# A diffusion backbone on one core: three modulation chunks move from TensorE to VectorE, and the rest is tied to its place

## The chip, the cores and the metric

The kernel runs on one core of one Trainium2 chip. The metric is the device time of one execution in microseconds; the time before is the median of three executions.

## The reference

Two layers of a diffusion backbone over 256 latent tokens and 256 context tokens, 2048 channels, float32. Each layer is a token mixer and then a gated MLP with a centred depthwise convolution of width 3. Every sub-layer reads a normalised and modulated stream. Layer 0 mixes by centred pooling in four channel groups, layer 1 by neighbourhood attention. Cut to what matters:

```python
ml = (silu_c  @ w_mod[i] + b_mod[i]).reshape(B, 6, 1, D)      # latent stream
mc = (silu_cc @ w_mod[i] + b_mod[i]).reshape(6, 1, 1, D)      # context stream
a_lat = modulate(rms_norm(h, norm1_g[i]), ml[:, 0], ml[:, 1]) # x * (1 + scale) + shift
# layer 0: window mean minus itself, then a 512 x 512 product per group
y_lat = pool_mix(a_lat, pool_w[j], pool_b[j], pool_scale[j])
h = h + ml[:, 2] * y_lat
h = h + ml[:, 5] * conv_ffn(modulate(rms_norm(h, norm2_g[i]), ml[:, 3], ml[:, 4]),
                            ffn_w_gate[i], ffn_w_up[i], ffn_conv_w[i], ffn_conv_b[i], ffn_w_down[i])
```

The context stream hc goes the same way with mc. For each layer the modulation is a vector of 2048 for each stream times a 2048 x 12288 matrix: six vectors (shift, scale and gate of the first norm, then of the second).

## The kernel before, in words

Channels lie on the partitions in 16 tiles (KT) of 128, hl and hc holding the two streams. Large products run in pairs of rounded float32 halves: a weight tile is loaded by SP's queue (load), cast on ScalarE into a high part and subtracted on VectorE into a low part (split, lines 172 and 174), and each product is three matmuls.

**The modulation of layer 0.** w_mod's 12288 columns are cut into 24 chunks of 512; chunk 4*w + g is vector w of channel group g (w = 3 is the second norm's shift, so chunks 12 to 15). mod_pe makes a chunk on TensorE: four pieces of two loads each (128 x 1024, 512 KB), and after each second piece a batch of 16 matmuls in four column strips (line 240), which waits until its four loads are whole. After the second batch ScalarE copies the accumulator (line 255), four transposes (line 262) bring it onto partitions, and VectorE adds up and applies bias and gain (lines 264, 217, 219). mod_pe is a generator with one pump step per piece. mods() puts the chunks in order: for each group g the chunks g, 4 + g, 8 + g, 16 + g, 12 + g, then 20 to 23, so 96 steps. need(n) pumps up to step n. shifts(g) copies a finished chunk 12 + g into the small tile sh (line 531). Layer 1's modulation is made later, while the MLP runs, by mod_pairs: VectorE adds up w_mod row by row (lines 298 and 300), transposes and reduces (310 and 311), and TensorE sums four quarters (quarter_sum, line 201).

**The partial stage.** The second norm's scale over channels is known only when all four groups have been mixed, so the MLP's first eight output tiles (NS, two products each, gate and up) are begun group by group without the norm: partial(g) multiplies group g's unnormalised tiles Ad (lines 705 to 707, 12 matmuls per output tile and product) and adds the result into part (line 718, VectorE). The norm's factor is applied at the end (late), and the shift's share of the product comes from its own small products pw of the weights with sh (line 687), transposed at line 721. While partial(g) runs, between(half) is called 32 times, once every six matmuls; each call pumps the modulation up to a step that grows with half (LEAD, RATE, PMAX), lets the next group's mixer take a step when its chunks are there (todo), lends buffers to the loads (lend, LENT), and in group 3 makes the second norm's factor (n2.rstd) and starts the normalised tiles A (normalise) and the first gates (GATES). The mixer of group g + 1 makes window sums on VectorE, its products on TensorE (lines 574 to 576), adds on GpSimd (line 635) and makes the Ad of the next group (lines 645 and 646).

**Order.** The program is emitted in this order, and a planner then orders each engine's instructions by a simulated time and by priorities. tc.issue_after(x) keeps an instruction behind x on the same engine; behind_of holds such an x for the modulation on TensorE, and is empty in the partial stage before. Loads are issued by SP in turn, each as soon as its buffer is free.

Of the kernel before, what the change touches and what calls it, by code (L numbers as in the profile page):

```python
# [33 lines left out]
LEAD = 18  # L34
RATE = 20
PMAX = 30

# [22 lines left out]
def kernel(ctx: ExitStack, tc: tile.TileContext, xT, cxT, wmod, wg, wu, wd, wp,  # L60
# [96 lines left out]

    casts = []

    def split(ts, name, share=0, keep=False):  # L160

        parts = []
        for j, (t, n) in enumerate(ts):
# [5 lines left out]
            with ExitStack() as behind:  # L169
                for ins in hold:  # L170
                    behind.enter_context(tc.issue_after(ins))
                casts.append(nc.scalar.copy(hi[:, :n], t[:, :n]).ins)  # L172
                eng = nc.gpsimd if share and turn[0] % share == 0 else nc.vector
                eng.tensor_tensor(lo[:, :n], t[:, :n], hi[:, :n].bitcast(F32), op=ALU.subtract)  # L174
            parts.append((hi, lo))
# [148 lines left out]
    class Norm:  # L324
# [51 lines left out]

        def rstd(self):
            nj = self.n // P
            ps = bank("d", f"{self.name}s")
# [9 lines left out]
            for j in range(nj):  # L389
                nc.vector.tensor_scalar(dg[:, P * j : P * j + P], ident, v[:, j : j + 1], None, op0=ALU.mult)  # L390
            pb = bank("d", f"{self.name}b")
            nc.tensor.matmul(pb[:, : self.n], ones, dg[:, : self.n], start=True, stop=True)
            return pb
# [36 lines left out]
    with ExitStack() as ph0:  # L430
# [64 lines left out]
        with ExitStack() as phs:  # L495
# [37 lines left out]
            def mods():  # L533

                for g in range(4):
                    for w in (0, 1, 2, 4):
                        yield from mod_pe(0, 4 * w + g, sc, f0)
                    yield from mod_pe(0, 12 + g, sc, f0)
                    shifts(g)
                for q in range(4):  # L540
                    yield from mod_pe(0, 20 + q, sc, f0)

            pump0 = mods()
            done = [0]

            def need(n):
                while done[0] < n:
                    next(pump0, None)
                    done[0] += 1
# [110 lines left out]
            def partial(g, sh, between):  # L660

                step = 0
                for fa in range(0, NS, 4):
                    for q, (nm, wsrc) in enumerate((("g", wg), ("u", wu))):
# [12 lines left out]
                        for j in range(4):  # L677
                            f = fa + j
                            between(2 * step)
                            if j == (3 if fa == 0 and q == 0 else 0):  # L680
                                need(20 * g + 21)
                                assert g in READY
# [19 lines left out]
                            for i in range(4):  # L702
# [3 lines left out]
                                nc.tensor.matmul(ps, hi[:, c : c + P], xl, start=False, stop=False)  # L706
                                nc.tensor.matmul(ps, lo[:, c : c + P], xh, start=False, stop=(final and i == 3))
                                if i == 1:
# [33 lines left out]
            with tc.issue_after(fetched[-1]):  # L742
                nc.sync.dma_start(vt[1], vec[:, NFIRST:])
            rstd = None
            for g in range(4):
                if g < 3:
                    lend((range(8, KT), [*range(12, KT), *range(4)], range(8))[g])
                mix = mixer(g + 1) if g < 3 else None
                todo = [20 * g + 20 + n for n in STEPS] if g < 3 else []
                last = [14]  # L750
# [3 lines left out]
                def between(half):  # L754
                    need(min(20 * g + LEAD + RATE * (half + 1) // 32, 20 * g + LEAD + PMAX))
                    if (g, half) in LENT:
                        lend(LENT[g, half])
                    if g == 3 and half == NRH:
                        nc.scalar.copy(rstd, n2.rstd())
                        late_norm.append(rstd)  # L760
                        need(20 * g + 21)
                    if todo and done[0] > todo[0] and half >= last[0] + 2:
                        last[0] = half
                        todo.pop(0)
                        next(mix)
                    k = (half - NRH) // 2
                    if g == 3 and 0 <= k < 12 and (half - NRH) % 2 == 0:
# [8 lines left out]
                for n in todo:  # L776
                    need(n)
                    next(mix)
            need(97)
            in_turn.clear()  # L780
# [768 lines left out]
```

## Time and the profile before

| | us |
|---|---|
| median of 3 executions | 3037.05 |
| lowest, highest | 3035.22, 3038.11 |
| the profiled execution, its own time | 3037.08 |
| its span, first to last instruction | 3035.3 |
| TensorE busy in the span | 2972.4 |
| mean granted TensorE clock | 0.995 |

The profile is one execution. PE is TensorE's matmuls, PEld its weight loads, DVE VectorE, ACT ScalarE, POOL GpSimd, SP the queue that issues the loads. A row of the timeline gives start, length, engine, line, operation, output <- inputs, and in brackets how long the engine stood idle before it and what released it. A clock of 1.00 is full speed.

### The profile page before, as it was taken

What the parts mean: (1) busy time and instruction counts of PE and PEld (TensorE: products, weight loads), DVE (VectorE), ACT (ScalarE), POOL (GpSimd) and SP (SyncE); (2) the same over time, 40 slices, a digit from 0 to 9 for tenths busy, and PEclk for the clock granted to TensorE, in tenths of its full rate; (3) what the DMA queues carried; (4) which work ended last, traced back from release to release, by engine and by line L of the source; (5) the groups of instructions that cost most, each with busy time, mean ns of one, the idle gap of its engine ahead of it and who ended that gap; (6) DMA issues with size and microseconds to landing.
All of it is one profiled execution on the core that took longest, in us unless ns stands there. A gap on an engine that the chain in (4) does not pass through costs nothing.

```text
span 3035.3 us, 40942 instructions
## 1 busy us (share of the span) xinstructions
PE 2972.4 (98%) x15132; PEld 2414.0 (80%) x15132; DVE 1943.6 (64%) x2782; ACT 1380.5 (45%) x2237; POOL 833.1 (27%) x819
## 2 busy tenths in 40 slices
PE   5999999999999999999999999999999999999998
PEld 2666568888888888888888887878888888888887
DVE  5455664386584857758485657474778666666666
ACT  4433454323333242333434534343556666566665
POOL 0000213303123030311305002020002566566665
PEclk9999999999999999999999999999999999999999
DMA  9798563374665847566482333333345555555563
GB/s 395 290 366 306 209 209 103 109 252 146 208 197 168 245 140 236 156 205 203 156 254 82 127 100 122 107 120 112 106 158 195 185 193 191 190 183 187 183 192 119
DMA packets 178935, 561.81 MB, mean 185 GB/s; under 512 B 17712, under 2 KB 22576, under 8 KB 178736
## 3 DMA queue, kind: packets, MB, share of 16 engines
q1 hardware_dynamic: 178736, 559.19, 56.5%
q8 instruction: 120, 1.97, 0.3%
q14 instruction: 79, 0.65, 0.1%
HBM read 557.03 MB, written 2.10 MB: 184 GB/s over the span
## 4 chain that ended last, share of the span: by engine, by line
PE 88%; issue 6%; DMA 2%; POOL 1%; DVE 1%; ACT 1%; SPq 0%; DVEq 0%; POOLq 0%; ACTq 0%
PE d L863 5%; PE d L864 5%; PE d L865 5%; PE u L1070 5%; PE g L1070 5%; PE d L1123 4%; PE g L807 4%; PE g L805 4%; PE g L806 4%; PE u L807 4%; PE u L805 4%; PE u L806 4%; PE u L1073 3%; PE g L1073 3%; PE d L1127 2%
## 5 line engine op out<-in xcount | busy, mean ns | idle before, releaser
L876 POOL TENSOR_TENSOR hl<-hl,dy 128x256 f32<-128x256 f32 x160 | 146.1, 913 | 945.8 <-ACT dy L875 945.6
L1139 POOL TENSOR_TENSOR hl<-hl,dy 128x256 f32<-128x256 f32 x320 | 332.1, 1075 | 188.3 <-ACT dy L1137 186.0
L300 DVE SCALAR_TENSOR_TENSOR macc<-wm,sc,macc 128x512 f32<-128x512 f32 (+1 forms) x360 | 328.7, 943 | 75.3 <-DMA wm<-wmod 74.3
L875 ACT ACTIVATE dy<-d,modT 128x256 f32<-128x256 f32 x320 | 133.1, 469 | 187.3 <-PE d L865 168.9
L876 POOL TENSOR_TENSOR hc<-hc,dy 128x256 f32<-128x256 f32 x160 | 129.4, 809 | 0.0
L174 DVE TENSOR_TENSOR wd_2l<-wd,wd_2h 128x1024 fp32r<-128x1024 f32 (+1 forms) x44 | 55.7, 1271 | 108.1 <-ACT wd_2h L172 106.9
L1137 ACT ACTIVATE dy<-d,modT 128x512 f32<-128x512 f32 x160 | 104.5, 684 | 43.0 <-PE d L1127 41.4
L240 PE MATMUL mod<-wm,sc 128*32 128x512 f32 x768 | 99.6, 629 | 9.9 <-DMA wm<-wmod 9.9
L1225 POOL TENSOR_TENSOR rk<-rk,rp 128x256 f32<-128x256 f32 x16 | 14.8, 926 | 324.0 <-DVE rk L1224 225.6
L174 DVE TENSOR_TENSOR wd_3l<-wd,wd_3h 128x1024 fp32r<-128x1024 f32 (+1 forms) x44 | 53.4, 1234 | 77.1 <-ACT wd_3h L172 75.7
L635 POOL TENSOR_TENSOR hl<-hl,pz 128x256 f32<-128x256 f32 x12 | 9.8, 820 | 286.9 <-ACT pz L633 286.9
L174 DVE TENSOR_TENSOR wd_1l<-wd,wd_1h 128x1024 fp32r<-128x1024 f32 (+1 forms) x44 | 53.7, 1225 | 53.3 <-ACT wd_1h L172 53.3
L172 ACT CAST wd_1h<-wd 128x1024 fp32r<-128x1024 f32 (+1 forms) x44 | 45.3, 1031 | 72.3 <-PE u L806 47.1
L174 DVE TENSOR_TENSOR wd_0l<-wd,wd_0h 128x1024 fp32r<-128x1024 f32 (+1 forms) x44 | 54.5, 1247 | 36.9 <-ACT wd_0h L172 36.9
L1314 ACT ACTIVATE sb<-sb,nm 128x512 f32<-128x512 f32 x64 | 46.3, 723 | 58.9 <-DVE nm L1310 57.3
L172 ACT CAST wd_0h<-wd 128x1024 fp32r<-128x1024 f32 (+1 forms) x44 | 45.0, 1031 | 54.5 <-PE u L1070 29.1
L1102 DVE TENSOR_TENSOR actb<-sgb,actb 128x256 fp32r<-128x256 f32 x43 | 50.8, 1180 | 26.0 <-ACT actb L1101 26.0
L480 ACT ACTIVATE sg<-g 128x512 f32<-128x512 f32 x43 | 27.2, 632 | 88.4 <-DVE g L477 88.3
L863 PE MATMUL d<-act,wd_2h 128*128 128x512 f32 x172 | 67.1, 390 | 0.0
L864 PE MATMUL d<-act,wd_2h 128*128 128x512 f32 x172 | 66.9, 389 | 0.0
L865 PE MATMUL d<-act,wd_2l 128*128 128x512 f32 x172 | 66.9, 389 | 0.0
L864 PE MATMUL d<-act,wd_0h 128*128 128x512 f32 x172 | 66.9, 389 | 0.0
(1778 smaller groups left out, 9304.8 us busy)
## 6 DMA issues: line engine op xcount, KB each, us to landing
wm<-wmod SPq DMA_DIRECT2D x384, 512.0 KB, 6.5
wd<-wd SPq DMA_DIRECT2D x168, 512.0 KB, 4.4
wg<-wg SPq DMA_DIRECT2D x156, 512.0 KB, 4.7
wu<-wu SPq DMA_DIRECT2D x156, 512.0 KB, 4.6
wv<-wv SPq DMA_DIRECT2D x32, 512.0 KB, 4.0
wk<-wq SPq DMA_DIRECT2D x32, 512.0 KB, 3.9
wq<-wq SPq DMA_DIRECT2D x32, 512.0 KB, 3.8
wo<-wo SPq DMA_DIRECT2D x32, 512.0 KB, 4.4
```

The costliest lines, as they stand in the source:

```text
L174: eng.tensor_tensor(lo[:, :n], t[:, :n], hi[:, :n].bitcast(F32), op=ALU.subtract)
L300: nc.vector.scalar_tensor_tensor(acc[s], v, sc2[:, k, s : s + 1], acc[s], op0=ALU.mult, op1=ALU.add)
L805: nc.tensor.matmul(ps, hi[:, c : c + P], xh, start=(k == 0), stop=False)
L806: nc.tensor.matmul(ps, hi[:, c : c + P], xl, start=False, stop=False)
L807: nc.tensor.matmul(ps, lo[:, c : c + P], xh, start=False, stop=(k == KT - 1))
L863: nc.tensor.matmul(ps, hi[:, o : o + P], xh, start=(i == 0), stop=False)
L864: nc.tensor.matmul(ps, hi[:, o : o + P], xl, start=False, stop=False)
L865: nc.tensor.matmul(ps, lo[:, o : o + P], xh, start=False, stop=(i == n - 1))
L876: nc.gpsimd.tensor_tensor(h_of(s)[:, k, :], h_of(s)[:, k, :], y[:, s], op=ALU.add)
L1070: nc.tensor.matmul(ps, hi[:, c : c + P], flat(B[k]), start=(k == 0), stop=False)
L1073: nc.tensor.matmul(ps[:, T:], lo[:, c : c + P], B[k][:, 0], start=False, stop=(k == KT - 1))
L1139: nc.gpsimd.tensor_tensor(hl[:, k, :], hl[:, k, :], y[:, q], op=ALU.add)
```

## The change

Chunks 13, 14 and 15 no longer go through mod_pe. added_up makes them on VectorE during partial(0), partial(1) and partial(2): 16 rows of 512 columns for each of the two streams, each row a multiply-add into the accumulator macc0 (a seventh tile of the ring act), then per stream a transpose and a reduction, and quarter_sum on TensorE. The rows are kept behind the last low-part subtraction that VectorE was given (vector_last). It takes a step every 0.8 half-steps, from half-step 10 in group 0 and from 3 in groups 1 and 2. mods() then has 84 steps, 16 for each of the groups 1 to 3; the pace is 20 steps per group in group 0 and 16 after. behind_of now always holds the last matmul of the partial products, so that modulation matmuls and transposes stay behind the place at which they are emitted. The second norm's factor is made in two parts, the sums and the diagonal at half-step 3 and the spreading matmul, tied in the same way, at half-step 5; the normalised tiles start one step later, and group 3 no longer waits for chunk 15.

```diff
@@ -32,8 +32,8 @@
 NC = 6
 
 LEAD = 18
-RATE = 20
-PMAX = 30
+RATE0 = 20
+RATE = 16
 
 NRH = 3
 GATES = (16, 19, 22, 25)
@@ -156,6 +156,7 @@
         return ts
 
     casts = []
+    vector_last = []
 
     def split(ts, name, share=0, keep=False):
 
@@ -171,7 +172,9 @@
                     behind.enter_context(tc.issue_after(ins))
                 casts.append(nc.scalar.copy(hi[:, :n], t[:, :n]).ins)
                 eng = nc.gpsimd if share and turn[0] % share == 0 else nc.vector
-                eng.tensor_tensor(lo[:, :n], t[:, :n], hi[:, :n].bitcast(F32), op=ALU.subtract)
+                ins = eng.tensor_tensor(lo[:, :n], t[:, :n], hi[:, :n].bitcast(F32), op=ALU.subtract)
+                if eng is nc.vector:
+                    vector_last[:] = [ins.ins]
             parts.append((hi, lo))
         if not keep:
             used(ts)
@@ -375,6 +378,10 @@
             return pb
 
         def rstd(self):
+            self.diagonal()
+            return self.spread_all()
+
+        def diagonal(self):
             nj = self.n // P
             ps = bank("d", f"{self.name}s")
             for i, sq in enumerate((self.acc, self.last)):
@@ -388,8 +395,14 @@
             dg = self.pool.tile([P, 512], F32, tag="t2", name=f"{self.name}d")
             for j in range(nj):
                 nc.vector.tensor_scalar(dg[:, P * j : P * j + P], ident, v[:, j : j + 1], None, op0=ALU.mult)
+            self.dg = dg
+
+        def spread_all(self, last=()):
             pb = bank("d", f"{self.name}b")
-            nc.tensor.matmul(pb[:, : self.n], ones, dg[:, : self.n], start=True, stop=True)
+            with ExitStack() as behind:
+                for x in last:
+                    behind.enter_context(tc.issue_after(x))
+                nc.tensor.matmul(pb[:, : self.n], ones, self.dg[:, : self.n], start=True, stop=True)
             return pb
 
     A = {}
@@ -535,10 +548,45 @@
                 for g in range(4):
                     for w in (0, 1, 2, 4):
                         yield from mod_pe(0, 4 * w + g, sc, f0)
-                    yield from mod_pe(0, 12 + g, sc, f0)
-                    shifts(g)
+                    if g == 0:
+                        yield from mod_pe(0, 12, sc, f0)
+                        shifts(0)
                 for q in range(4):
                     yield from mod_pe(0, 20 + q, sc, f0)
+
+            def added_up(ch, acc):
+
+                for k in range(KT):
+                    if k % 2 == 0:
+                        g, j = divmod(k, 4)
+                        ts = load(lambda a, b: wmod[0, ch, g, :, 512 * j + a : 512 * j + b], 1024, f"wv{ch}_{k}")
+                        t = ts[0][0]
+                    with ExitStack() as behind:
+                        for x in vector_last:
+                            behind.enter_context(tc.issue_after(x))
+                        v = t[:, 512 * (k % 2) : 512 * (k % 2) + 512]
+                        for s in both:
+                            if k == 0:
+                                nc.vector.tensor_scalar(acc[:, s], v, sc2[:, k, s : s + 1], None, op0=ALU.mult)
+                            else:
+                                nc.vector.scalar_tensor_tensor(acc[:, s], v, sc2[:, k, s : s + 1], acc[:, s],
+                                                               op0=ALU.mult, op1=ALU.add)
+                    if k % 2:
+                        used(ts)
+                    yield
+                r = st.tile([P, 16, 2], F32, tag="modr", bufs=2, name=f"modr0_{ch}")
+                for s in both:
+                    t = f0.tile([P, 512], F32, tag="t2", name=f"modu{s}_0_{ch}")
+                    nc.vector.transpose(t, acc[:, s])
+                    nc.vector.tensor_reduce(out=r[:, :, s], in_=t.rearrange("p (k r) -> p k r", r=32), axis=AX.X, op=ALU.add)
+                    yield
+                yield
+                with ExitStack() as behind:
+                    for x in behind_of:
+                        behind.enter_context(tc.issue_after(x))
+                    src = quarter_sum(r, 2, f"modt_0_{ch}")
+                finish_mod(0, ch, both, src)
+                shifts(ch - 12)
 
             pump0 = mods()
             done = [0]
@@ -678,7 +726,8 @@
                             f = fa + j
                             between(2 * step)
                             if j == (3 if fa == 0 and q == 0 else 0):
-                                need(20 * g + 21)
+                                if g == 0:
+                                    need(21)
                                 assert g in READY
                                 pw = bank("d", f"pw{nm}{g}_{fa}")
                                 for i in range(4):
@@ -704,7 +753,8 @@
                                 xh, xl = flat(A[4 * g + i][:, 0]), flat(A[4 * g + i][:, 1])
                                 nc.tensor.matmul(ps, hi[:, c : c + P], xh, start=(first and i == 0), stop=False)
                                 nc.tensor.matmul(ps, hi[:, c : c + P], xl, start=False, stop=False)
-                                nc.tensor.matmul(ps, lo[:, c : c + P], xh, start=False, stop=(final and i == 3))
+                                ins = nc.tensor.matmul(ps, lo[:, c : c + P], xh, start=False, stop=(final and i == 3))
+                                behind_of[:] = [ins.ins]
                                 if i == 1:
                                     between(2 * step + 1)
                             step += 1
@@ -742,28 +792,39 @@
             with tc.issue_after(fetched[-1]):
                 nc.sync.dma_start(vt[1], vec[:, NFIRST:])
             rstd = None
+            summed = act_tile("macc0", F32)
             for g in range(4):
                 if g < 3:
                     lend((range(8, KT), [*range(12, KT), *range(4)], range(8))[g])
                 mix = mixer(g + 1) if g < 3 else None
-                todo = [20 * g + 20 + n for n in STEPS] if g < 3 else []
+                todo = [16 * g + 20 + n for n in STEPS] if g < 3 else []
+                adding = [added_up(13 + g, summed)] if g < 3 else []
+                taken = [0]
                 last = [14]
                 F = {}
                 rstd = n2.acc
 
                 def between(half):
-                    need(min(20 * g + LEAD + RATE * (half + 1) // 32, 20 * g + LEAD + PMAX))
+                    if g == 0:
+                        need(LEAD + RATE0 * (half + 1) // 32)
+                    else:
+                        need(LEAD + 4 + RATE * g + RATE * (half + 1) // 32)
+                    while adding and (half - (3 if g else 10)) * 10 >= 8 * taken[0]:
+                        taken[0] += 1
+                        if next(adding[0], "end") == "end":
+                            adding.pop()
                     if (g, half) in LENT:
                         lend(LENT[g, half])
                     if g == 3 and half == NRH:
-                        nc.scalar.copy(rstd, n2.rstd())
+                        n2.diagonal()
+                    if g == 3 and half == NRH + 2:
+                        nc.scalar.copy(rstd, n2.spread_all(behind_of))
                         late_norm.append(rstd)
-                        need(20 * g + 21)
                     if todo and done[0] > todo[0] and half >= last[0] + 2:
                         last[0] = half
                         todo.pop(0)
                         next(mix)
-                    k = (half - NRH) // 2
+                    k = (half - NRH) // 2 - 1
                     if g == 3 and 0 <= k < 12 and (half - NRH) % 2 == 0:
                         normalise(0, 3, h_of, both, rstd, f0, range(k, k + 1), keep=F)
                     if g == 3 and half == 24:
@@ -776,7 +837,8 @@
                 for n in todo:
                     need(n)
                     next(mix)
-            need(97)
+            need(85)
+            behind_of.clear()
             in_turn.clear()
             nbank[0] = 0
             A.update(F)

```

## The prediction

> **What bounds the kernel now.** I read the page first, then the busy time by stage, PE's timeline in the partial stage, the waits, and VectorE's timeline.
>
> ```profile
> span 3035.3 us, 40942 instructions
> PE 2972.4 (98%) x15132; PEld 2414.0 (80%) x15132; DVE 1943.6 (64%) x2782; ACT 1380.5 (45%) x2237; POOL 833.1 (27%) x819
> PE 88%; issue 6%; DMA 2%; POOL 1%; DVE 1%; ACT 1%; SPq 0%; DVEq 0%; POOLq 0%; ACTq 0%
> ```
>
> PE is busy for 98% of the span and makes 88% of the chain that ended last. Work taken from PE in the stage that changes shortens the run, unless PE then waits. That stage runs from 69 to 417 us. Its first three groups are cut in two below; the last row is the head of group 3. Columns: stretch, length, busy time of PE, PEld, DVE, ACT and POOL (instructions in brackets), granted clock, DMA share, GB/s.
>
> ```profile
> 69.40:107.76 38.36, 37.60 (x237) 22.68 (x237) 13.11 (x24) 16.67 (x31) 0.00 (x0) 1.00 1.02 393
> 107.76:158.20 50.44, 48.02 (x281) 32.48 (x280) 28.30 (x55) 24.21 (x45) 6.28 (x8) 1.00 0.66 229
> 158.20:194.00 35.80, 35.58 (x205) 23.07 (x205) 12.89 (x26) 9.09 (x15) 0.00 (x0) 0.95 1.01 389
> 194.00:246.00 52.00, 52.00 (x313) 32.98 (x311) 35.47 (x69) 21.92 (x41) 6.39 (x8) 1.00 0.79 280
> 246.00:280.70 34.70, 34.70 (x213) 22.09 (x209) 14.15 (x27) 9.38 (x16) 0.00 (x0) 1.00 1.00 372
> 280.70:331.10 50.40, 49.45 (x293) 32.46 (x293) 36.15 (x70) 21.61 (x41) 5.95 (x8) 1.00 0.72 264
> 331.10:376.50 45.40, 39.05 (x221) 24.63 (x219) 26.86 (x55) 15.44 (x35) 10.53 (x8) 0.92 0.59 202
> ```
>
> PE is full in groups 0 to 2. The DMA engines are full in the first half of each group and free for a fifth to a third of the second. VectorE works 140.1 of 261.7 us in the three groups (the six rows added), so 121.6 us are idle. Group 3's head is where PE loses most: 6.4 us idle and a clock of 0.92.
>
> **What comes off PE.** Chunks 13 to 15 lose their matmuls and transposes. One batch of 16 matmuls, and one set of four transposes, in PE's timeline:
>
> ```profile
> 270.09 0.60 PE L262 MATMUL modt<-ident,modev 128*128 128x128 f32 x4
> 270.62 1.92 PE L240 MATMUL mod<-wm,sc 128*32 128x512 f32 x16
> ...
> 276.46 0.39 PE L707 MATMUL cu<-Ad,wcu_0l 128*128 128x512 f32 x1
> 276.78 1.92 PE L240 MATMUL mod<-wm,sc 128*32 128x512 f32 x16
> 278.64 0.50 PE L705 MATMUL cu<-Ad,wcu_0h 128*128 128x512 f32 x1
> 278.98 0.40 PE L706 MATMUL cu<-Ad,wcu_0h 128*128 128x512 f32 x1
> 279.22 0.40 PE L707 MATMUL cu<-Ad,wcu_0l 128*128 128x512 f32 x1
> ```
>
> From L707 at 276.46 to L707 at 279.22 are 2.76 us. Three steps between ordinary matmuls take 0.23 us each (the pitch of undisturbed neighbours, about the 0.24 of the last two rows), so one batch costs 2.07 us. The transposes cost 0.53 (270.09 to 270.62). A chunk is two batches and one set, 4.67 us; three are 14.0 us. All of it stands in PE's full stretches. Each chunk now ends with a sum over four quarters on PE, which layer 1 already shows:
>
> ```profile
> L201 PE MATMUL modt_0s<-modr,quad x2: 191/232/274, 637.6 to 637.6; 128*128 128x32 f32 x2
> ```
>
> Two matmuls of 0.23 are 0.46 us, 1.4 for three; at the lower bound they vanish between neighbours. I take 1.4. Net: 12.6 us less.
>
> **Two waits that lose their cause.** Group 3 now has the last batch of chunk 15 in front of its first shift sums:
>
> ```profile
> 343.54 0.16 DVE L386 TENSOR_SCALAR n2v<-n2v 128x4 f32<-128x4 f32 x1
> 345.18 3.64 PE L240 MATMUL mod<-wm,sc 128*32 128x512 f32 x16 [4.64 <-DMA wm<-wmod]
> 345.34 0.86 DVE L390 TENSOR_SCALAR n2d<-ident,n2v 128x128 f32<-128x128 f32 x4
> 348.75 2.02 PE L392 MATMUL n2b<-n2d,ones 128*128 128x512 f32 x2
> 355.32 0.16 DVE L531 COPY sh<-modT 128x8 f32<-128x8 f32 x1
> 355.63 1.09 PE L687 MATMUL pwg<-wcg,sh 128*32 128x256 f32 x16 [1.65 <-ACT A L405]
> ...
> 345.20:350.60 5.40, 5.40 (x18) 1.37 (x19) 1.01 (x5) 0.00 (x0) 0.00 (x0) 0.50 0.97 333
> ```
>
> PE stands 4.64 us for that batch's weights and then runs 5.4 us at a clock of 0.50, 2.7 us lost: together 7.3. The shift of group 3 is copied at 355.32, and pwg, which reads it, starts right after, 1.65 us late (the view names ACT, but that copy came last). After the change chunk 15 is summed during group 2 and need(81) is gone, so these 9.0 us lose their cause.
>
> What is late next there is the second norm. Its diagonal is ready at 346.2 (345.34 and 0.86), because L386 came only at 343.54; from there the chain is 2.7 us long. The spreading matmul is now tied two half-steps after the sums: 12 matmuls of 0.23 and a batch of 2.07, 4.8 us of cover. If L386 comes as promptly as that needs, the wait is nothing; if it is again held up, the chain from the sums to the diagonal,
>
> ```profile
> 337.13 0.28 PE L382 MATMUL n2s<-ones,n2q 128*128 128x1 f32 x2
> ```
>
> is 9.1 us against 4.8, a wait of 4.3 and half a slow stretch like the one above, 6.5 in all. I take 3.3, the middle: nothing in the rows says which. Later normalisation by one step and the last 14 of 84 pump steps in group 3 cost nothing: PE's own matmuls hide them.
>
> **What VectorE gets.** A chunk is 32 rows, two transposes and two reductions, all seen in layer 1:
>
> ```profile
> 602.99 4.71 DVE L300 SCALAR_TENSOR_TENSOR macc<-wm,sc,macc 128x512 f32<-128x512 f32 x7
> L310 DVE STREAM_TRANSPOSE modu<-macc x32: 657/682/705, 626.0 to 1636.5; 128x512 f32<-128x512 f32 x32
> L311 DVE TENSOR_REDUCE modr<-modu x32: 634/654/677, 627.2 to 1638.4; 128x16 f32<-128x512 f32 x32
> DVE macc L300 <- DMA wm<-wmod: 74.3, 63, 4.0
> ```
>
> Seven rows take 4.71 us, 0.67 each; 32 are 21.5, the rest 2.7: 24.2 us a chunk, 72.6 for three. Of 121.6 us idle 49.0 remain, and 36.4 once PE's share of the stage is 12.6 shorter. So the work fits, in groups 1 and 2 in half-steps 3 to 19, before the mixers crowd the second half.
>
> The new wait is that of a row for its weights. Behind it in VectorE's queue stand the additions into part (L718) that free PE's accumulators, the splits, and the mixer. Layer 1 waits 1.2 us a time (74.3 over 63); 24 loads at that are 28.3 us, inside the 36.4. So I charge PE only where slack is short: at the change of groups, where PE waits for Ad.
>
> ```profile
> 158.20 0.73 PE L705 MATMUL cg<-Ad,wcg_0h 128*128 128x512 f32 x2 [2.42 <-ACT Ad L645]
> 158.20:162.60 4.40, 4.17 (x11) 2.98 (x12) 3.61 (x9) 2.65 (x7) 0.00 (x0) 0.64 0.96 336
> ```
>
> That gap is 2.4 us and 4.4 us at a clock of 0.64, 1.6 more: 4.0. There are three changes of group. Between none of them and three extra gaps (12.0), and 4.0 of gain if this one goes, I take one, 4.0.
>
> On the clock the Trainium skill ("TensorE: Matmul & The Clock Gate", Part 1) says that it drops after an idle window of some 3.4 us. By that rule the 2.4 us gap would have cost itself alone and the sum would be 1.6 lower; the trace shows a clock of 0.64 behind 2.42 us, and the measurement decides.
>
> The 24 loads replace 24 loads, so bytes stay. Group 0 gets chunk 13's 4.2 MB (8 loads of 128 x 1024 fp32) on top of what it had; SP's queue puts them ahead of wp and wcg. The row 107.76 to 158.2 moves 229 GB/s where the first moves 393: 8.3 MB of room. Three evictions fewer on ACT and the tie itself (an order on PE that the trace mostly has already) I cost at nothing; PE's matmuls hide the first, and where the tie makes a transposed chunk late it is one of the gaps above.
>
> **Sum.** The profiled execution took 3037.08 us, the median is 3037.05. 3037.08 - 12.6 - 9.0 + 3.3 + 4.0 = 3022.8, so 3023.
>
> **Rivals.** *All gaps go.* With the norm prompt and the gap at 158.2 closed by the earlier mixer: 3037.08 - 12.6 - 9.0 - 4.0 = 3011.5. For it: groups 1 and 2 have 16 pump steps instead of 20, so by the code their mixers start some three half-steps earlier. Against: VectorE is fuller.
>
> *The gaps come back.* The norm waits 6.5 and each change of group has one more gap: 3015.5 + 6.5 + 12.0 = 3034.0, no change that a measurement tells (it tells 0.2%, 6 us). For it: VectorE's rows fill just the idle time that kept the boundary short.
>
> *VectorE's queue stands.* Weights come late to the row at its head, additions behind it stop, and PE runs out of accumulators.
>
> ```profile
> ACT wcg_4h L172 <- DMA wcg<-wg: 19.8, 6, 7.1
> ```
>
> In this stage a cast that waits for weights waits 3.3 us (19.8 over 6). 24 loads at 3.3 are 79.2, 42.8 above the 36.4 idle: 3015.5 + 42.8 = 3058. It decides from a mean wait of 1.5 us per load, and is slower by over 0.2% from 2.7. For it: DMA share 1.0 in half-steps 3 to 16. Against: the row counts six such waits in the whole stage, and layer 1's rows wait 1.2 us a time.
>
> *POOL slows.*
>
> ```profile
> 155.21 1.29 POOL L635 TENSOR_TENSOR hl<-hl,pz 128x256 f32<-128x256 f32 x1 [4.61 <-ACT pz L633]
> 156.47 0.72 POOL L635 TENSOR_TENSOR hc<-hc,pz 128x256 f32<-128x256 f32 x1
> ```
>
> The residual additions take 0.72 us, and 1.29 beside VectorE work. All 24 slowed by 0.57 and on the path give 13.7: 3022.8 + 13.7 = 3036.5. The new rows end before the mixer's additions in groups 1 and 2, so it is unlikely. The Trainium skill ("GPSIMD Engine Reference", Specifications) says that both engines share SBUF interfaces and contend when a VectorE instruction has two SBUF inputs, as every new row but a chunk's first two has; the two rows above agree.
>
> **How the numbers follow.** Forecast, 3015 to 3031: 0.48. All gaps gone: 0.17. Gaps back: 0.12. POOL: 0.02. VectorE's queue: 0.21. Faster is 0.48 + 0.17 = 0.65, within 0.2% 0.14, slower 0.21. The range starts at 3010, under the best case, and ends at 3046, a mean wait of some 2.8 us, which leaves out about half of the slow case.
>
> **What would show it.** Right: 42 sets of mod matmuls instead of 48 and 84 transposes instead of 96; no PE wait for wm in group 3; pwg there without a wait; VectorE over 80% busy in groups 1 and 2; PE idle under 12 us between 69 and 405 us. Wrong: L718 late behind macc0 rows that wait for wv, PE waiting for DVE; or n2b on PE's waits.

## The result, and the profile after

The changed kernel takes 3049.71 us (median of 5, 3047.94 to 3052.96); the kernel before takes 3037.05 (5, 3034.09 to 3040.96). The ratio is 1.0044, interval 1.0033 to 1.0055: 12.7 us slower, where 14 us less were forecast. The profiled execution took 3050.51 us.

The page after, its span, engines and chain:

```profile
span 3048.7 us, 40880 instructions
PE 2968.1 (97%) x15030; PEld 2412.5 (79%) x15030; DVE 2015.3 (66%) x2896; ACT 1379.8 (45%) x2234; POOL 834.6 (27%) x819
PE 88%; issue 4%; DVE 3%; DMA 3%; POOL 1%; ACT 1%; SPq 0%; DVEq 0%; POOLq 0%; ACTq 0%
```

PE is busy 4.3 us less and the span is 13.4 us longer. So PE waits more: DVE and DMA have 3% of the chain each, where they had 1% and 2%.

Busy time by stage, one row for each group, from the group's first product to the next group's, the last to the first product of the down projection (columns as in the prediction). First the kernel after, then before's last group, whose other three can be added up from the prediction's rows:

```profile
70.19:170.79 100.60, 89.22 (x518) 55.79 (x518) 67.37 (x126) 41.05 (x77) 6.37 (x8) 0.98 0.93 348
170.79:262.37 91.58, 84.54 (x467) 54.70 (x467) 68.14 (x129) 30.47 (x55) 6.47 (x8) 0.96 0.70 261
262.37:358.88 96.51, 86.84 (x466) 55.28 (x467) 71.78 (x137) 32.69 (x60) 6.47 (x8) 0.93 0.74 266
358.88:453.64 94.76, 93.36 (x517) 63.02 (x516) 77.64 (x137) 52.52 (x99) 18.83 (x13) 1.00 0.68 227
```

```profile
331.12:441.75 110.63, 102.14 (x537) 66.12 (x535) 77.33 (x145) 55.21 (x105) 19.06 (x13) 0.95 0.66 225
```

Three sums can be read from such rows: PE's idle time (length less busy), what the lower clock costs (busy times one less the clock), and the rest, PE's work at full clock.

| us, groups 0 to 2 / group 3 | idle | slow clock | work |
|---|---|---|---|
| before | 4.4 / 8.5 | 1.8 / 5.1 | 255.6 / 97.0 |
| after | 28.1 / 1.4 | 11.2 / 0 | 249.4 / 93.4 |

Work fell by 9.8 us, group 3's losses (idle and slow clock) by 12.2; groups 0 to 2 lose 33.1 us more. So these stages together are 11.1 us longer, and another 2.3 us of the 13.4 lie outside them. PE's longest waits in these groups, in its timeline after:

```profile
132.68 0.50 PE L754 MATMUL cu<-Ad,wcu_4h 128*128 128x512 f32 x1 [4.18 <-ACT wcu_4h L173]
170.79 1.65 PE L754 MATMUL cg<-Ad,wcg_0h 128*128 128x512 f32 x3 [5.33 <-ACT Ad L693]
237.09 1.09 PE L736 MATMUL pwu<-wcu,sh 128*32 128x256 f32 x16 [2.24 <-DVE pug L778]
276.07 0.68 PE L265 MATMUL modt<-ident,modev 128*128 128x128 f32 x4 [3.01 <-ACT wcu_0h L173]
326.90 0.73 PE L622 MATMUL pm<-ph,wp3h 128*128 128x512 f32 x2 [2.65 <-ACT ph L656]
331.83 1.96 PE L736 MATMUL pwu<-wcu,sh 128*32 128x256 f32 x16 [2.13 <-DVE pug L778]
```

L754, L736, L265 and L622 are the L705, L687, L262 and L574 of before; L693 is its L645. None of these waits but the change at L754 stood in the kernel before, and they name five different things. At the head of group 3, where before lost most, nothing waits any more:

```profile
365.19 0.95 PE L389 MATMUL n2s<-ones,n2acc 128*128 128x1 f32 x8
366.00 1.03 PE L389 MATMUL n2s<-ones,n2q 128*128 128x1 f32 x8
372.77 1.02 PE L405 MATMUL n2b<-n2d,ones 128*128 128x512 f32 x2
373.72 1.09 PE L736 MATMUL pwg<-wcg,sh 128*32 128x256 f32 x16
```

VectorE writes the norm's diagonal 2.5 us ahead of the spreading matmul that reads it:

```profile
369.43 0.88 DVE L397 TENSOR_SCALAR n2d<-ident,n2v 128x128 f32<-128x128 f32 x4 [0.18 <-POOL n2v L394]
```

The mod matmuls of 69 to 455 us, in the groups by line, after and then before (count; busy, mean ns; idle before them):

```profile
L243 PE MATMUL mod<-wm,sc 128*32 128x512 f32 x544 | 66.2, 599 | 0.0
```

```profile
L240 PE MATMUL mod<-wm,sc 128*32 128x512 f32 x640 | 80.5, 610 | 4.6 <-DMA wm<-wmod 4.6
```

### The profile page after: what moved, and what is told of

Same layout as the page of the kernel before. It is cut to its first block, busy times and chain, and to the rows that moved or that the text cites. A ratio compares the mean times of both kernels' runs of the same rounds, so it can differ in the third digit from the quotient of the medians.

```text
span 3048.7 us, 40880 instructions
## 1 busy us (share of the span) xinstructions
PE 2968.1 (97%) x15030; PEld 2412.5 (79%) x15030; DVE 2015.3 (66%) x2896; ACT 1379.8 (45%) x2234; POOL 834.6 (27%) x819
## 4 chain that ended last, share of the span: by engine, by line
PE 88%; issue 4%; DVE 3%; DMA 3%; POOL 1%; ACT 1%; SPq 0%; DVEq 0%; POOLq 0%; ACTq 0%
PE d L925 5%; PE d L926 5%; PE u L1132 5%; PE d L927 5%; PE g L1132 5%; PE d L1185 4%; PE u L867 4%; PE u L869 4%; PE u L868 4%; PE g L869 4%; PE g L867 4%; PE g L868 4%; PE u L1135 3%; PE g L1135 3%; PE d L1189 2%
## 5 line engine op out<-in xcount | busy, mean ns | idle before, releaser
L1287 POOL TENSOR_TENSOR rk<-rk,rp 128x256 f32<-128x256 f32 x16 | 14.8, 926 | 324.0 <-DVE rk L1286 225.6
L683 POOL TENSOR_TENSOR hl<-hl,pz 128x256 f32<-128x256 f32 x12 | 10.3, 862 | 305.0 <-ACT pz L681 303.1
L243 PE MATMUL mod<-wm,sc 128*32 128x512 f32 x672 | 84.8, 621 | 5.6 <-DMA wm<-wmod 5.6
L572 DVE SCALAR_TENSOR_TENSOR macc<-wv,sc,macc 128x512 f32<-128x512 f32 x90 | 63.6, 750 | 16.5 <-DMA wv<-wmod 16.4
```

## The experiments

All were timed in five rounds beside the kernel before (3037 to 3038 us in each job); each ratio is to it. Line numbers differ by a few between kernels. "Without the tie" means that behind_of stays empty in the partial stage.

**1. The change taken apart.** The tie alone on the kernel before; the change without the tie; the change with short rows, which add up 32 of 512 columns and so leave out most of the second norm's shifts of groups 1 to 3; and the change with only chunk 15 on VectorE.

```diff
 e1, on before:
+                                behind_of[:] = [ins.ins]
 e2, on after:
-                                behind_of[:] = [ins.ins]
 e3, on after:
-  ...scalar_tensor_tensor(acc[:, s], v, ..., acc[:, s],
+  ...scalar_tensor_tensor(acc[:, s, 0:32], v[:, 0:32], ..., acc[:, s, 0:32],
 e4, on after (chunks 13, 14 by mod_pe again, pace 20 in groups 0 to 2):
-                adding = [added_up(13 + g, summed)] if g < 3 else []
+                adding = [added_up(15, summed)] if g == 2 else []
```

Tie alone. Expected:

> The kernel before with the tie alone: behind_of always holds the last partial matmul, all 24 chunks stay on TensorE. Theory V (VectorE's row work crowds the mixer and its PE waits are the loss): the tie hardly matters, 3033 to 3041 us, group 3 keeps its wait of about 4.6 us for wm. Theory T (the tie makes TensorE wait at its place): 3045 us or more, with new waits of TensorE between 100 and 350 us. Theory P (the loads' new order and pace are late): as before, 3037.

Without the tie. Expected:

> The changed kernel without the tie: behind_of stays empty in the partial stage. V: still 3045 to 3055 us, TensorE's waits for ScalarE's ph and Ad and for VectorE's pug stay. T: the new waits go, 3015 to 3028. P: 3045 to 3055, with the waits for weights.

Short rows. Expected:

> The changed kernel with each multiply-add row but the first cut from 512 to 32 columns; loads, waits for them and order stay, so the shifts of groups 1 to 3 leave out most columns. About 90 rows shrink from 0.67 us of pitch to about 0.2, so VectorE loses some 45 us of work. V: 3015 to 3028 us, the waits between 100 and 350 us mostly gone. T: 3045 to 3055, since TensorE's ties are as they were. P: 3042 to 3055, since the 24 loads and the waits of the rows for them are as they were.

Chunk 15 alone. Expected:

> Only chunk 15 goes to VectorE (in group 2); chunks 13 and 14 are back on TensorE with the pace of before in groups 0 to 2, tie and split norm as in the changed kernel. V: a third of the row work and so about a third of the new loss of 34 us (12.7 slower, 12.6 of work and 9.0 of waits gone): 3037 - 4.2 - 9.0 + 11 = 3035 us, with groups 0 and 1 as full as before. T: the tie acts in all groups, 3045 or more. P: a third of the loads moved, 3035, with the loss in waits for weights.

Measured: the tie alone 3046.91 us (1.0020 to 1.0045), 8.8 slower. Without the tie 3035.16 (0.9985 to 1.0003): the tie is worth 14.5 us of the change, more than the whole 12.7, and what is left measures as no change. T had named the tie, but its 3015 to 3028 without it did not come. Short rows 3042.80 (1.0010 to 1.0028), 6.9 better than the change, where V had 3015 to 3028. Chunk 15 alone, tied, 3038.09 (0.9992 to 1.0010), under T's 3045 and over the 3035 of V and P.

The change without the tie, by group:

```profile
69.74:166.86 97.12, 90.47 (x535) 56.77 (x535) 65.22 (x125) 40.88 (x77) 6.74 (x8) 0.98 0.95 359
166.86:252.93 86.07, 82.01 (x466) 54.04 (x466) 69.04 (x133) 30.36 (x55) 6.49 (x8) 0.98 0.77 282
252.93:344.63 91.70, 83.04 (x471) 53.99 (x467) 71.52 (x136) 32.34 (x60) 6.48 (x8) 0.98 0.75 281
344.63:437.12 92.49, 91.21 (x502) 63.19 (x499) 75.44 (x135) 51.80 (x98) 18.95 (x13) 1.00 0.69 230
```

Idle and slow clock are 8.5, 5.7 and 10.3 us in groups 0 to 2, against 13.2, 10.4 and 15.8 with the tie: about five us in each group, none in group 3. How that comes about shows at the change to group 1. PE's timeline there, first after, then without the tie:

```profile
162.37 0.66 PE L265 MATMUL modt<-ident,modev 128*128 128x128 f32 x4 [0.34 <-ACT modev L258]
162.95 1.92 PE L243 MATMUL mod<-wm,sc 128*32 128x512 f32 x16
164.81 0.65 PE L771 MATMUL ptu<-ident,peu 128*128 128x128 f32 x4
170.79 1.65 PE L754 MATMUL cg<-Ad,wcg_0h 128*128 128x512 f32 x3 [5.33 <-ACT Ad L693]
```

```profile
161.11 0.60 PE L265 MATMUL modt<-ident,modev 128*128 128x128 f32 x4
161.64 1.92 PE L243 MATMUL mod<-wm,sc 128*32 128x512 f32 x16
163.49 0.66 PE L770 MATMUL ptu<-ident,peu 128*128 128x128 f32 x4
164.08 1.92 PE L243 MATMUL mod<-wm,sc 128*32 128x512 f32 x16
166.86 0.96 PE L754 MATMUL cg<-Ad,wcg_0h 128*128 128x512 f32 x3 [0.85 <-ACT Ad L693]
```

In both PE has nothing of its own to do until Ad is there. Without the tie a second batch, whose weights have landed, is drawn forward and fills 1.9 us; with the tie it belongs behind a product of group 1 and can't come. The other part of the 5.33 us is VectorE's. Its timeline after, from the reduction of the last chunk (L267) to the first Ad that it writes (some rows left out, marked ...):

```profile
164.78 0.19 DVE L267 TENSOR_REDUCE modT<-modt 128x8 f32<-128x32 f32 x1
164.88 1.00 DVE L572 SCALAR_TENSOR_TENSOR macc<-wv,sc,macc 128x512 f32<-128x512 f32 x1
165.81 1.21 DVE L345 TENSOR_TENSOR n2acc<-n2acc,n2q 128x512 f32<-128x512 f32 x1
166.94 0.74 DVE L572 SCALAR_TENSOR_TENSOR macc<-wv,sc,macc 128x512 f32<-128x512 f32 x1
167.61 0.15 DVE L220 TENSOR_TENSOR modT<-modT,vt 128x8 f32<-128x8 f32 x1
...
168.97 0.75 DVE L572 SCALAR_TENSOR_TENSOR macc<-wv,sc,macc 128x512 f32<-128x512 f32 x1 [0.51 <-DMA wv<-wmod]
169.64 0.16 DVE L222 SCALAR_TENSOR_TENSOR modT<-modT,vt 128x8 f32<-128x8 f32 x1
...
171.64 0.48 DVE L694 SCALAR_TENSOR_TENSOR Ad<-hl,modT,Ad 128x256 fp32r<-128x256 f32 x1
```

Three small operations that Ad waits for (L267, L220, L222) stand between row additions of 0.7 us, additions to n2acc and a wait of 0.51 us for a row's weights. The first Ad that PE reads is ScalarE's, which starts when L222 is done: at 169.84, 5.1 us after L267 starts, against 3.2 (162.67 to 165.90) without the tie. It isn't the number of rows: without the tie four rows stand between, here three, with two additions to n2acc and the wait. L267 itself is 2.1 us later here, behind transposes that PE makes 1.3 us later (162.37 and 161.11).

Tied alone on the kernel before, the wait moved: the batch of 345.18 no longer stands there, and the unsplit norm waits instead, 5.68 us, with nothing drawn forward to cover it. That is only a part of the 8.8 us: by groups this run is 3.1, -1.4, 3.4 and 3.3 us longer than before.

```profile
353.67 2.07 PE L392 MATMUL n2b<-n2d,ones 128*128 128x512 f32 x2 [5.68 <-DVE n2d L390]
```

**2. What is tied.** The batches alone (transposes and quarter sums free), the transposes and quarter sums alone (the norm's spreading matmul stays tied in both), a tie that is 36 matmuls looser, and a tie that is lifted for the first four half-steps of groups 1 to 3.

```diff
 e9, on after, in the transposes (and none for quarter_sum):
-            for x in behind_of:
+            for x in () if done[0] > LEAD else behind_of:
 e10, on after: the same edit in the batches
 e13, on after:
-                                behind_of[:] = [ins.ins]
+                                recent.append(ins.ins)
+                                behind_of[:] = recent[-13:-12]
 e14, on after:
-                                behind_of[:] = [ins.ins]
+                                behind_of[:] = [ins.ins] if g == 0 or step > 1 else []
```

Batches. Expected:

> The changed kernel with the tie kept for the modulation's batches of 16 matmuls and the norm's spreading matmul, and taken off the transposes and quarter sums. Changed 3049.7, without any tie 3035.2. Theory F (a tied batch can no longer fill a wait of TensorE, such as the one for Ad at a change of group, so the batches carry the loss): 3045 to 3050. Theory L (tied transposes come late, and with them the modulation that the next group's Ad needs): 3035 to 3040.

Transposes. Expected:

> The other half: transposes and quarter sums tied, batches free. F: 3034 to 3039. L: 3045 to 3050.

Looser. Expected:

> The changed kernel with the tie loosened: a batch stays behind the partial matmul that stands 36 matmuls (six half-steps, 8 us) before its place. Theory F (tied batches cannot come early to fill a wait): a batch may now come up to 8 us early, so most of the 14.5 us come back, 3035 to 3040. If only the order as such matters and not how early a batch may come: 3047 to 3051.

Lifted at the change. Expected:

> The changed kernel with the tie lifted in half-steps 0 to 3 of groups 1 to 3 and kept elsewhere. If the loss sits at the change of groups, in the wait for Ad of 5.3 us: 3039 to 3043. If it is spread over the groups: 3045 to 3049.

Measured: batches 3049.32 (1.0022 to 1.0049), the whole loss; transposes 3041.07 (1.0002 to 1.0020), 5.9 above no tie; the looser tie 3035.80 (0.9986 to 1.0004), all 14 us back; lifted at the change 3051.73 (1.0032 to 1.0058), nothing back.

So it is how early the tied work may come that matters, not that it is tied: with 36 partial matmuls of room it can be drawn into a wait. At 0.23 each these are 8 us, but a group is 192 of them in 86.0 us (group 1 of that run), so the room is some 16 us; less was not tried. The run loosens every tie at once, batches and transposes. For the batches alone theory F has what it expected (3045 to 3050). The tied transposes cost 5.9 us where F allowed at most 4, so L holds for a smaller part. The two parts do not add up: either alone would do harm.

The last run doesn't settle where the loss sits. At the change to group 1 it has two batches instead of one (32 mod matmuls between the transposes and ptu), and PE's gap shrinks from 5.33 to 3.78 us:

```profile
170.25 1.88 PE L754 MATMUL cg<-Ad,wcg_0h 128*128 128x512 f32 x3 [3.78 <-ACT Ad L693]
```

But Ad came no earlier to speak of (170.25, after 170.79, without the tie 166.86), and the idle time of the whole stage stayed at 29.5 us. Inside group 1 it lost what the batch had gained: that group is 96.4 us long, 4.9 more than after, at a clock of 0.91. So the run does not show that the changes of group are free of loss. The profiles after and without the tie say more: the tie adds 8.7 us of idle time in groups 0 to 2, of which the gap at that change makes 4.5. The other half lies inside the groups, such as the wait for ph (2.65 us), which is not there without the tie.

**3. What is left without the tie.** The next group's mixer held back three half-steps in groups 1 and 2, with and without the tie; short rows without the tie, and with the mixer held back as well (both leave out the same columns as above).

```diff
 e5, e6 (e5 without the tie):
-                last = [14]
+                last = [17 if g else 14]
 e7, e12: e2 and e5, each with the edit of e3
```

Expected, in the order e5, e6, e7, e12:

> The changed kernel without the tie (3035.16 us), with the mixers of groups 2 and 3 held back to the half-steps of the kernel before (steps from half-step 19 instead of 16). Theory M (the new pace starts the mixer three half-steps earlier, its products meet the shift sums ptg and pwu, and the accumulator ring d runs out behind VectorE's pug): the waits of pwu for pug (2.05 and 2.97 us, each with a slow stretch) and of pm for ph go, 3024 to 3030 us. Theory V (row work on VectorE): they stay or grow, 3033 to 3040.

> The changed kernel, tie included, with the same hold on the mixers of groups 2 and 3. M: 8 to 12 us under the changed kernel, 3038 to 3042. T (tie) with V: 3046 to 3053, since neither is touched.

> Without the tie and with each multiply-add row but the first cut from 512 to 32 columns (the shifts of groups 1 to 3 leave out most columns). With the tie the short rows gave 3042.8 against 3049.7. If tie and row work add up: 3035.2 - 7 = 3028. V alone: 3016 to 3022, all of the saved 12.6 and 9.0 us shows. M: 3026 to 3034, the waits of pwu for pug stay.

> No tie, mixers held back, and rows but the first cut to 32 columns (the shifts of groups 1 to 3 leave out most columns). If the three causes add up (14.5 for the tie, 3.3 for the mixer, 6 for the row work): 3024 to 3027. If row work and mixer overlap, 3028 to 3031.

Measured: mixer late without the tie 3031.86 (0.9967 to 0.9985), with the tie 3046.07 (1.0017 to 1.0036): 3.3 and 3.6 us, about the same with and without the tie, though with it the interval overlaps that of the change (1.0033 to 1.0055). Theory M had more, 8 to 12 us with the tie. Short rows 3029.59 (0.9957 to 0.9981), 5.6 better than e2; both together 3028.48 (0.9954 to 0.9979), 6.7 better than e2, less than 3.3 and 5.6 added.

Held back, the mixer no longer meets the pw products, and the waits for pug (2.05 and 2.97 us in e2) are gone from PE's waits. Short rows also end a wait in group 0. ScalarE's cast of the weights that PE waits for there, in e5 and then in e7:

```profile
133.81 1.04 ACT L173 CAST wcu_4h<-wcu 128x1024 fp32r<-128x1024 f32 x1
```

```profile
130.12 1.03 ACT L173 CAST wcu_4h<-wcu 128x1024 fp32r<-128x1024 f32 x1
```

The loads are the same in both, yet with short rows the cast comes 3.7 us earlier and PE's wait of 4.26 us (e5) isn't there. So it isn't the bytes alone: chunk 13's full rows are part of what makes these weights late. The trace of e5 shows the way. The cast has no wait of its own, but stands in ScalarE's order right behind that of the mixer's ph, which waits for VectorE's pf:

```profile
133.28 0.62 ACT L656 CAST ph<-pf 128x512 fp32r<-128x512 f32 x1 [4.33 <-DVE pf L653]
```

On VectorE, pf (132.57) stands behind full rows; with short rows pf is done by 125.3 and ph is cast at 125.32.

**4. Fewer chunks on VectorE, and elsewhere in time.** Chunk 15 alone without the tie; chunks 14 and 15 (e5 with 13 back on TensorE); the kernel before with a faster pace in group 2, so that its chunk 15 is done before group 3; and e5 and e8 with the rows begun at another half-step.

```diff
 e8, on e4:
-                                behind_of[:] = [ins.ins]
 e11, on e5 (with the need() and pace of chunk 13 on TensorE):
-                adding = [added_up(13 + g, summed)] if g < 3 else []
+                adding = [added_up(13 + g, summed)] if 0 < g < 3 else []
 e16, on before:
-  ... 20 * g + LEAD + RATE * (half + 1) // 32 ...
+  ... 20 * g + LEAD + (RATE + 3 * (g == 2)) * (half + 1) // 32 ...
 e15 and e17, on e5:
-                    while adding and (half - (3 if g else 10)) * 10 >= 8 * taken[0]:
+                    while adding and (half - (9 if g else 10)) * 10 >= 8 * taken[0]:   # e15
+                    while adding and (half - (0 if g else 10)) * 10 >= 8 * taken[0]:   # e17
 e18, on e8:
+                    while adding and half * 10 >= 8 * taken[0]:
```

Expected, in the order e8, e11, e16, e15, e17, e18:

> Only chunk 15 on VectorE, pace of before in groups 0 to 2, split norm, and no tie. T: the tie's loss (9 us on the kernel before) goes, so 3038.1 - 9 = 3029 or, if nothing new waits, 3037 - 4.2 - 9.0 = 3024. V: 3032 to 3036, the waits at the end of group 2 stay. M: no early mixer here, so 3024 to 3029.

> No tie, mixers held back as in the run with 3031.9 us, and chunk 13 back on TensorE: only chunks 14 and 15 on VectorE, group 0 and 1 paced as before. Theory G (in group 0 the added chunk's loads and rows cost more than its batch: the wait of cu for wcu_4h, 4.3 us and its slow stretch, and the rows in front of group 1's modulation): 3031.9 + 4.7 - 8 = 3026 to 3030. Without G, the batch comes back and nothing goes: 3035 to 3038.

> The kernel before with nothing but a faster pace in group 2 (23 pump steps instead of 20), so that chunk 15 is finished on TensorE before group 3 begins; no rows on VectorE, no tie. If the two waits at the head of group 3 (4.64 with its slow stretch, and 1.65, together 9 us) come from chunk 15's place: 3027 to 3031. If the weights are simply late there: 3036 to 3039, with the wait moved to the end of group 2.

> No tie, mixers held back (3031.9), and the rows of groups 1 and 2 start at half-step 9 instead of 3. Theory Q (rows at the head of VectorE's queue, waiting for their weights, stand in front of the modulation and the Ad of the new group): the waits for Ad and for part early in the groups go, 3026 to 3029. Theory V: rows meet the mixer's window sums, 3033 to 3040.

> The version without the tie and with the mixers held back (3031.9), its rows of groups 1 and 2 begun at half-step 0 instead of 3. Theory V (rows cost time where they meet the window sums of the next mixer, so the sooner they end the better): of the 3.4 us that shortened rows gained in that version some part comes back, 3029 to 3031.5, and no longer wait for window sums than there. Rival H (the head of a group is VectorE's short place too: the new group's low parts and additions stand behind rows that wait for weights): a gap of some 2.5 us and its slow stretch at each of the two heads, 3036 to 3040, with waits of TensorE for cu or cg parts in the first 10 us of groups 1 and 2.

> The version with only chunk 15 on VectorE and no tie (3032.1), that chunk's rows begun at half-step 0 of group 2 instead of 3. Theory V: 3030 to 3032, at most 2 us better since only one group has rows. Rival H: 3034 to 3036, one gap and its slow stretch at the head of group 2.

Measured: chunk 15 without the tie 3032.10 (0.9967 to 0.9986), 6.0 better than tied; two chunks 3033.15 (0.9978 to 0.9996), no gain over three; the faster pace 3039.41 (1.0000 to 1.0017), no gain; rows late 3043.00 (1.0008 to 1.0025), rows early 3042.17 (1.0006 to 1.0024), both 10 to 11 us worse than e5; chunk 15 with early rows 3028.95 (0.9963 to 0.9980), the best version that leaves nothing out.

Two of these moved a loss rather than removed it. With two chunks, group 0 is 9.0 us shorter than in e5 (91.6 against 100.6), so chunk 13 does cost there, but group 1 is 9.5 longer (91.0 against 81.5). With the faster pace PE waits neither for wm nor at pwg at the head of group 3, and group 3 takes 100.1 us instead of 110.6; so those two waits do come from chunk 15's place. But group 2 takes 93.5 instead of 85.0.

With rows late, PE waits at the end of the chunk:

```profile
324.77 0.64 PE L204 MATMUL modt_15s<-modr,quad 128*128 128x32 f32 x2 [5.02 <-DVE modr L581]
```

The rows have run into the window sums of the next mixer. With the pace raised on the kernel before, which has no row and no tie, the wait for pug shows up at the end of group 2, as it did in the change:

```profile
315.04 1.96 PE L687 MATMUL pwu<-wcu,sh 128*32 128x256 f32 x16 [2.99 <-DVE pug L728]
```

The pace starts the next mixer earlier, so by the code this is the earlier mixer again, by itself. Rows early cost what they gained by another way. The waits of VectorE for weights, over 69 to 431 us (total, times, longest), after, in e5 and with rows early:

```profile
DVE macc L572 <- DMA wv<-wmod: 16.4, 11, 4.3
```

```profile
DVE macc L572 <- DMA wv<-wmod: 8.5, 6, 3.1
```

```profile
DVE macc L572 <- DMA wv<-wmod: 3.4, 1, 3.4
```

PE at the change to group 1 with rows early:

```profile
173.75 0.97 PE L754 MATMUL cg<-Ad,wcg_0h 128*128 128x512 f32 x3 [3.15 <-ACT Ad L693]
```

Begun early, the rows wait in one place only, but PE waits 3.15 us for Ad at the change to group 1 (e5 waits 0.85 us there), much as theory H of the expectations has it. Summed as in the table above, the profiled stage is 10.7 us longer than in e5: 2.9 of idle time, some 6 of slower clock and 1.8 of work. The gap is most of the first; why the clock was lower in groups 1 to 3 stays open. One chunk does not show this cost: with chunk 15 alone an early start was, if anything, better (0.9972 against 0.9976 in another job, intervals overlapping). H had 3034 to 3036 there and V 3030 to 3032. Neither theory holds for both runs, and no rule for the start of three chunks' rows follows.

## Why the prediction was wrong

**The step that failed** is the half sentence "the tie itself (an order on PE that the trace mostly has already) I cost at nothing". It costs 14.5 us here and 8.8 alone. Read as an order it is true: the batches stood between products in the trace before. But that order was made by the planner out of what was ready, and the freedom to draw a batch forward is what kept PE full: 0.2 us idle in the whole of group 1 before. A batch is 2 us of work that depends on nothing but its weights. Tied to its place, it can't stand in for a late Ad, or in e1 for a late diagonal of the norm. The prediction looked for what the tie would make late (a transposed chunk), which is the smaller part: 5.9 us for the transposes, the whole loss for the batches. That the batches must not come early is shown by the runs (tied, free, and 36 matmuls looser); which waits each of them would have covered is read from the profiles at two places only.

**Work off PE**: -12.6 forecast, -9.8 in the profile of the change, -11.0 without the tie (352.6 to 341.6). Right in kind, a little large. The stage has x544 mod matmuls where before has x640: six sets of 16 fewer, as expected, and their 4.6 us of waiting for weights are gone.

**Group 3**: -9.0 and +3.3 forecast, -12.2 measured. No wait for wm, none at pwg. So this group gained 6.5 us more than the net 5.7. The norm's wait did not come: from the last row of sums at 366.00 to the finished diagonal at 370.31 are 4.3 us, not the 9.1 of before, and the spreading matmul stands 6.8 us after that row. The middle of the bounds was the wrong choice; in e1 the unsplit norm with a tie waits 5.68 us and then runs 5.3 us at a clock of 0.71, 1.5 more, so something like the upper bound does occur. That bound of 6.5 does not come out of its rows either: 4.3 and half of the 2.7 us lost in the stretch above it are 5.7, the middle 2.8, and the sum would have been 3022.3.

**The gaps**: +4.0 forecast, 33.1 measured in groups 0 to 2. From after to e2, 14.8 of these are the tie's. Without it 18.3 are left, still far over 4.0, so the charge of one extra gap was too small as well. Of these, e5 ends the pug waits for 3.3 us and e7 shows 5.6 as the rows' share, 6.7 together (e12); the other 11.6 are not accounted for by any run. The earlier mixer is a step with the wrong sign, in the rival "All gaps go": mixers that start earlier were counted for a gain, and they cost. They run beside pw there, and in the kernel both take their accumulators from the same ring (d).

**"So the work fits"** on VectorE was read from idle time, and in time it does fit: VectorE was 74% busy in groups 1 and 2, not over 80%, because these groups got longer (over the 172.9 us that they took before it would be 81%). What it hid is where the idle time lies. Rows late and rows early are both 10 us worse than a start at half-step 3, with the same total.

**The rival "VectorE's queue stands"** named an engine that has a part in the loss, and the wrong size. Rows did wait, 16.4 us in 11 waits, where it said 79; over 24 loads that is 0.7 us each, under the 1.5 from which it decides, and its 42.8 us never came. The kernel is slower for another reason: the 0.21 for slower was given to this mechanism alone, and the tie had no rival of its own. POOL's rival did not come: POOL is busy 19.3 us in groups 0 to 2, where before it was 18.6.

**What ends it**: e5, e8 and e18 drop the tie: 3031.9, 3032.1 and 3029.0 us, 0.24 to 0.28% under the kernel before. e5 keeps all of the work taken off PE and about half of group 3's gain (6.3 us lost there, where before it was 13.6), e8 and e18 a part of the work and nearly all of that gain (1.3 and 1.4 lost). That is still short of the 3023 of the sum, and e12, whose rows are a sixteenth as wide, only reaches 3028.5. Its profile says where the rest is: the work fell by 9.6 us instead of 12.6, idle time and slow clock came to 18.7 us where the forecast's terms leave 18.0, and 2.9 us lie outside the stage. So of the 6.6 us by which that execution misses the sum, 3.0 are PE's work, forecast too high, 2.9 stand outside the stage, where the sum had nothing, and 0.7 are gaps.

## What to carry to other kernels

When work with no close consumer is pinned to its place on the busiest engine, cost the pin as the loss of a filler: list the waits that such work covers now, and assume they open. If an order must be kept, tie to something well earlier: here 36 partial matmuls of room, some 16 us, gave the whole loss back. And read idle time of the receiving engine by place, not by sum: the same rows cost 10 us more begun six half-steps later or three earlier.

## What was not expected of the hardware

The clock falls behind short gaps, but not behind each. Stretches of 5 us in the profile after, each begun where a gap ends (5.33 us, 2.24 and 3.01), and one of before behind a gap of 1.29 at 417.44:

```profile
170.79:175.79 5.00, 4.20 (x9) 2.90 (x10) 5.00 (x12) 3.39 (x7) 0.00 (x0) 0.50 0.18 70
237.09:242.09 5.00, 4.30 (x29) 2.89 (x30) 0.84 (x2) 2.81 (x7) 1.76 (x3) 1.00 0.38 134
276.07:281.07 5.00, 5.00 (x30) 2.75 (x34) 5.00 (x9) 0.59 (x1) 0.00 (x0) 0.66 0.98 338
```

```profile
417.40:422.20 4.80, 4.24 (x11) 3.03 (x12) 4.78 (x10) 4.20 (x7) 0.00 (x0) 0.65 0.48 186
```

A gap of 2.24 us left the clock at 1.00; one of 1.29, with 0.53 more a microsecond later, was followed by 0.65. So a gap's price can't be read from its length. Summed over the stage it is no steadier: 29.5 us of idle time came with 11.2 us of slow clock after, 12.9 with 6.9 before, 20.7 with 5.1 without the tie (e2) and 9.5 with 7.9 in e18, so from 0.25 to 0.8 us for each. A gap should be costed with something on top, but these runs give no fixed rate. The Trainium skill ("TensorE: Matmul & The Clock Gate", Part 1) has the clock fall after an idle window of some 3.4 us, and calls the window free-running. The spread of these rows agrees with a window that doesn't start with the gap; a fall behind 1.29 us does not agree with 3.4 us of idleness.
